# Projecting v and the output gate of a head together, 512 columns at a time

## The chip, the cores and the metric

The kernel runs on one core of a Trainium2 chip, as one launch. The metric is the device time in microseconds. The core's engines run side by side and meet at semaphores: TensorE (PE; matrix products into PSUM, and the loading of their stationary operand, PEld), VectorE (DVE), ScalarE (ACT), GpSimd (POOL) and SyncE (SP), which here only starts transfers.

## The reference

A trunk of two residual layers over 2048 tokens of width 1024: a chunked gated linear attention (GLA, 4 heads), then a causal convolution module, then one RMSNorm. The change touches the attention layer alone. Of that layer:

```python
proj = h @ w_in                       # h = rmsnorm(x, norm_w), (2048, 1024)
q, k, v, z, g_lr = jnp.split(
    proj, [GLA_DK, 2 * GLA_DK, 2 * GLA_DK + GLA_DV, 2 * GLA_DK + 2 * GLA_DV], axis=-1)
log_a = jax.nn.log_sigmoid((g_lr @ w_g2 + b_g).astype(jnp.float32)) / GLA_GATE_TAU
...
b = jnp.cumsum(log_a, axis=3)         # within a chunk of 64 tokens
q_dec = q * jnp.exp(b)
k_inv = k * jnp.exp(-b)
k_end = k * jnp.exp(b_last - b)
scores = jnp.where(causal, jnp.einsum('bhnid,bhnjd->bhnij', q_dec, k_inv), 0.0)
o_intra = jnp.einsum('bhnij,bhnjv->bhniv', scores, v)
# over the chunks: o_inter = q_dec @ S;  S = exp(b_last) * S + k_end^T v
...
o = o * lax.rsqrt(jnp.mean(o * o, axis=-1, keepdims=True) + EPS) * gn_w
o = o.reshape(B, T, GLA_DV) * jax.nn.silu(z)
x = x + o @ w_out
```

A head has 128 columns of q, 128 of k, 256 of v and 256 of z, the output gate.

## The kernel before

**Products.** Each float32 operand is split into a high and a low part (wh and wl for weights, ah and al for activations), and a product is the sum of three: high x high, high x low, low x high (`mm3`, line 144). `proj_f` takes 128 columns of the weights as the stationary operand and streams 512 tokens past them; q, k and the output projection go this way. `proj_t` takes 128 tokens as the stationary operand and streams 256 columns of the weights past them; v and z go this way. Either is 24 products (8 slices of the inner dimension, three each) into one PSUM bank.

**Weights.** The weight matrices are cut into units of 256 columns over all 1024 rows (8 KB per partition for each half of the split). A head has three: unit 3h for q and k, 3h+1 for v, 3h+2 for z; units 12 to 15 are the output projection, later ones belong to the convolution layer. `load_unit` brings one in two pieces of 512 KB: a transfer into `wr` (line 123, two buffers), a rounding copy on ScalarE to wh (124), a subtraction on GpSimd to wl (125; on VectorE for the first two units). wh and wl have two buffers each, and `next_unit` asks for one unit ahead.

**Order.** The sequence goes in two halves of 1024 tokens, each in two blocks of 512 (b = 0, 1) and eight groups of 128. `start_block` prepares a block: x is scaled and split (`prep_x`, 269 to 276), then `gate_low` makes the 16 columns of the gate's low rank (288; its weights `wgs` are split once at the start and stay in SBUF), the token norms (166 to 168, 178), and `gate` the factors E and Ei of a head (310 to 323). Then `head` runs over the four heads. `qk` makes q and k of a block and multiplies them by E and Ei out of PSUM (332, 338). `values` makes v of four groups (437, 438); all eight groups' v is kept (8 buffers). After that a loop over the eight groups makes z of a group (472) and issues the group's `core` in three stages, one unit of work apart: `scores` (379 to 383), `mix` (388 to 403) and `turn` (413 to 422). In head 0 of each half, block 0 has q, k and v made before block 1 is started. `out1` is the output projection with the residual, and starts block 0 of the next half (`ahead`).

**Banks.** PSUM's eight banks are in three groups: three of `mm` (projections), two of `pb`, three of `pm`. In head 0 v goes to `pb`, in the other heads to `mm`; `mix` uses `pb` throughout.

**What sets the order.** Tile's scheduler lists the instructions of each engine ahead of time, from their order in the program, their priorities (`tc.high_priority(offset=200)` moves those of `start_block` 200 places forward) and a simulated time line; a buffer is given out there as it comes free. On the chip each engine works through its list in order.

## Time and profile before

| | us |
|---|---|
| device time, median of 3 runs | 1694.59 (1694.3 to 1696.6) |
| span of the profiled execution | 1691.3 |
| TensorE busy in it | 1617.2 (96%) |
| VectorE | 1015.6 (60%) |
| GpSimd | 936.0 (55%) |
| ScalarE | 742.2 (44%) |

Times of instructions are from the span's start. The attention layer takes the first half of the span, to about 850 us, and the convolution layer the rest. Matmuls are pipelined: one's busy time overlaps the next one's, so that the cost of one in a full stream is the distance from start to start. A group of instructions is named by its line, engine, operation and output<-inputs; "idle before" is what the engine waited and for whom.

### The profile page before, as it was taken

What the parts mean: (1) busy time and instruction counts of PE and PEld (TensorE: products, weight loads), DVE (VectorE), ACT (ScalarE), POOL (GpSimd) and SP (SyncE); (2) the same over time, 40 slices, a digit from 0 to 9 for tenths busy, and PEclk for the clock granted to TensorE, in tenths of its full rate; (3) what the DMA queues carried; (4) which work ended last, traced back from release to release, by engine and by line L of the source; (5) the groups of instructions that cost most, each with busy time, mean ns of one, the idle gap of its engine ahead of it and who ended that gap; (6) DMA issues with size and microseconds to landing.
All of it is one profiled execution on the core that took longest, in us unless ns stands there. A gap on an engine that the chain in (4) does not pass through costs nothing.

```text
span 1691.3 us, 23564 instructions
## 1 busy us (share of the span) xinstructions
PE 1617.2 (96%) x9028; PEld 1413.4 (84%) x9028; DVE 1015.6 (60%) x1473; ACT 742.2 (44%) x1254; POOL 936.0 (55%) x795
## 2 busy tenths in 40 slices
...
GB/s 188 30 78 57 63 51 57 76 130 139 164 34 55 58 72 42 75 33 132 132 196 46 63 50 57 85 80 154 38 69 238 61 68 94 206 125 88 235 176 124
DMA packets 74015, 165.68 MB, mean 98 GB/s; under 512 B 7760, under 2 KB 16464, under 8 KB 73904
## 3 DMA queue, kind: packets, MB, share of 16 engines
...
q14 instruction: 41, 0.34, 0.1%
...
## 4 chain that ended last, share of the span: by engine, by line
PE 62%; DVE 16%; POOL 7%; DMA 6%; issue 4%; ACT 3%; SPq 0%; POOLq 0%; DVEq 0%; ACTq 0%
PE mm L144 52%; DVE pb L638 6%; PE pb L144 3%; DVE al L190 2%; DMA wr<-in_wall_dram 2%; PE pb L388 1%; POOL wl L125 1%; PE pb L390 1%; POOL convB L624 1%; DVE S L713 1%; PE pm L379 1%; POOL convA L624 1%; DVE d L734 1%; POOL b L736 1%; DVE pb L642 1%
## 5 line engine op out<-in xcount | busy, mean ns | idle before, releaser
L144 PE MATMUL mm<-ah,wh 128*128 128x512 f32 (+1 forms) x1600 | 599.1, 389 | 43.2 <-DVE u L761 10.7
L144 PE MATMUL mm<-al,wh 128*128 128x512 f32 (+1 forms) x1600 | 594.6, 387 | 1.7 <-DVE al L190 1.7
L144 PE MATMUL mm<-ah,wl 128*128 128x512 f32 (+1 forms) x1600 | 592.9, 387 | 2.3 <-POOL wl L125 2.3
L125 POOL TENSOR_TENSOR wl<-wr,wh 128x1024 fp32r<-128x1024 f32 x140 | 358.5, 2575 | 195.2 <-ACT wh L124 190.3
L144 PEld LDWEIGHTS mm<-ah,wh 128*128 128x128 f32 x1600 | 304.0, 191 | 109.0 <-DVE u L761 13.1
L144 PEld LDWEIGHTS mm<-ah,wl 128*128 128x128 f32 x1600 | 303.3, 191 | 62.4 <-POOL wl L125 4.2
L144 PEld LDWEIGHTS mm<-al,wh 128*128 128x128 f32 x1600 | 303.9, 191 | 59.7 <-DVE al L190 2.6
L144 PE MATMUL mm<-wh,ah 128*128 128x256 f32 x896 | 259.2, 289 | 0.0
L144 PE MATMUL mm<-wh,al 128*128 128x256 f32 x896 | 254.6, 284 | 0.0
L144 PE MATMUL mm<-wl,ah 128*128 128x256 f32 x896 | 254.2, 284 | 0.0
L124 ACT ACTIVATE wh<-wr 128x1024 fp32r<-128x1024 f32 x144 | 145.3, 1050 | 109.0 <-PE mm L144 78.9
L638 DVE SCALAR_TENSOR_TENSOR pb<-u,C,pb 128x512 f32<-128x512 f32 x252 | 183.8, 747 | 0.5
L638 DVE SCALAR_TENSOR_TENSOR pb<-u,dwc,pb 128x512 f32<-128x512 f32 x240 | 179.4, 748 | 1.6
L144 PEld LDWEIGHTS mm<-wl,ah 128*128 128x128 f32 x896 | 171.4, 191 | 0.4
L144 PEld LDWEIGHTS mm<-wh,ah 128*128 128x128 f32 x896 | 171.3, 191 | 0.4
L144 PEld LDWEIGHTS mm<-wh,al 128*128 128x128 f32 x896 | 171.3, 191 | 0.0
L622 ACT ACTIVATE prod<-u,C 128x512 f32<-128x512 f32 x148 | 105.6, 721 | 137.6 <-POOL convA L624 78.5
L624 POOL TENSOR_TENSOR convA<-convA,prod 128x512 f32<-128x512 f32 x74 | 99.5, 1344 | 6.6 <-ACT prod L622 3.0
L624 POOL TENSOR_TENSOR convB<-convB,prod 128x512 f32<-128x512 f32 x74 | 99.6, 1346 | 3.9 <-ACT convB L620 0.7
L397 DVE SCALAR_TENSOR_TENSOR S<-S,dec,pb 128x256 f32<-128x256 f32 x56 | 26.8, 479 | 95.4 <-PE pb L144 95.3
L401 POOL TENSOR_TENSOR ss<-ss,e 128x1 f32<-128x1 f32 x64 | 13.3, 208 | 124.5 <-ACT g L400 124.5
L523 DVE TENSOR_TENSOR Q<-mm,Q 128x512 f32<-128x512 f32 x32 | 22.0, 688 | 92.7 <-PE mm L144 78.9
...
## 6 DMA issues: line engine op xcount, KB each, us to landing
wr<-in_wall_dram SPq DMA_DIRECT2D x144, 512.0 KB, 4.1
...
```

What stands on the lines that cost most here:

```text
L124: act.activation(wh[:, ks, :], raw, AF.Copy)
L125: (dve if i < 2 else pool).tensor_tensor(wl[:, ks, :], raw, wh[:, ks, :].bitcast(F32), ALU.subtract)
L144: pe.matmul(ps, s, m, start=(i == 0), stop=(i == 3 * n - 1))
L190: dve.tensor_tensor(lo, src, hi.bitcast(F32), ALU.subtract)
L379: pe.matmul(s_ps[:, 0:192], ki[:, js], Q[:, j].rearrange("p s c -> p (s c)"), start=True, stop=True)
L388: pe.matmul(o_ps, Q[:, j, 0:2].rearrange("p s c -> p (s c)"), S[h], start=True, stop=False)
L390: pe.matmul(o_ps, x, y, start=first and n == 0, stop=n == 2)
L397: dve.scalar_tensor_tensor(S[h], S[h], dec[:, j:j + 1], kv, ALU.mult, ALU.add)
L523: dve.tensor_tensor(xr, ps, xr, ALU.add)
L622: act.activation(p, src, AF.Copy, scale=w)
L624: pool.tensor_tensor(acc, acc, p, ALU.add)
L638: dve.scalar_tensor_tensor(dstm, src, w, ps, ALU.mult, ALU.add)
```

## The change

v and z of a head become one projection of 512 columns. The weights of both lie side by side, and the two units now part the inner dimension: unit 3h+1 has its first 512 rows, unit 3h+2 the last 512, each of 512 columns (the same bytes). A group of 128 tokens is 24 products of 512 columns into one whole `mm` bank; v leaves the left half of the bank, Silu of z the right one, and the group's `core` stages follow at once. So v needs three buffers where it had eight. A wide pass holds both units from its first group to its last; units 0, 3, 6, 9 and 12 (q and k of each head, and the first of the output projection) get a pool of their own, `wq`, with one buffer. For the room this takes, `raw` has four buffers in place of five, and the gate's split weights no longer stay: they use a `wr` buffer, are written to DRAM once and read back for the three later blocks. In head 0, block 1 is started after the four groups of block 0; the gate of the next head is issued between groups 3 and 4.

```diff
...
 TAPS = 31
+UW = 2048
 HALO = 15
...
     order += list(range(28, 32)) * 4
+    LONE = {0, 3, 6, 9, 12}
     wstate = {"next": 0, "ready": []}
...
         u = order[i]
-        wh = wp.tile([P, KT, 256], F32R, name="wh")
-        wl = wp.tile([P, KT, 256], F32R, name="wl")
+        wpool = wq if u in LONE else wp
+        wh = wpool.tile([P, UW], F32R, name="wh")
+        wl = wpool.tile([P, UW], F32R, name="wl")
         wstate["ready"].append((u, wh, wl))
...
         def part(s):
-            ks = slice(4 * s, 4 * s + 4)
-            raw = wp.tile([P, 4, 256], F32, name="wr")
-            sp.dma_start(out=raw, in_=wall[u].rearrange("p (k c) -> p k c", c=256)[:, ks, :])
-            act.activation(wh[:, ks, :], raw, AF.Copy)
-            (dve if i < 2 else pool).tensor_tensor(wl[:, ks, :], raw, wh[:, ks, :].bitcast(F32), ALU.subtract)
+            cs = slice(s * UW // 2, (s + 1) * UW // 2)
+            raw = wp.tile([P, UW // 2], F32, name="wr", bufs=2)
+            sp.dma_start(out=raw, in_=wall[u][:, cs])
+            act.activation(wh[:, cs], raw, AF.Copy)
+            (dve if i < 2 else pool).tensor_tensor(wl[:, cs], raw, wh[:, cs].bitcast(F32), ALU.subtract)
...
-    def next_unit(expect):
-        while len(wstate["ready"]) < 2 and wstate["next"] < len(order):
+    def pop_unit(expect, ahead):
+        while len(wstate["ready"]) < ahead and wstate["next"] < len(order):
             load_unit()
...
         return wh, wl
+    def next_unit(expect):
+        return [w.rearrange("p (k c) -> p k c", c=256) for w in pop_unit(expect, 2)]
+    def next_wide(expect):
+        w = []
+        for s in range(2):
+            hl = [t.rearrange("p (k c) -> p k c", c=2 * DV) for t in pop_unit(expect + s, 3 - s)]
+            w += [(hl[0][:, k], hl[1][:, k]) for k in range(KT // 2)]
+        return w
...
     def proj_t(ps, w, a, j):
-        wh, wl = w
         s = slice(j * P, (j + 1) * P)
-        mm3(ps, [(a[k][0][:, s], a[k][1][:, s], wh[:, k, :], wl[:, k, :]) for k in range(KT)])
+        mm3(ps, [(a[k][0][:, s], a[k][1][:, s], w[k][0], w[k][1]) for k in range(KT)])
...
     l1 = ExitStack()
+    wq = l1.enter_context(tc.tile_pool(name="wq", bufs=1))
     s2 = l1.enter_context(tc.tile_pool(name="s2", bufs=1))
...
-    BUFS = {"raw": 5, "tmp": 3, "E": 2, "Ei": 2, "ki": 2, "kd": 1, "st": 4}
+    BUFS = {"raw": 4, "tmp": 3, "E": 2, "Ei": 2, "ki": 2, "kd": 1, "st": 4}
...
     S = [l1c.tile([P, DV], F32, name=f"S{h}") for h in range(HEADS)]
-    wgs = l1c.tile([P, KT, P], F32R, name="wgs")
     g2t = l1c.tile([96, HEADS * DK], F32R, name="g2t")
-    wgr = l1c.tile([P, KT, 16], F32, name="wgr")
+    wgd = tc.dram_tile((P, KT * P), F32, name="wg_scratch")
...
-    def load_small():
+    def gate_weights(first):
+        t = wp.tile([P, UW // 2], F32R, name="wr", bufs=2)
+        wgs = t.rearrange("p (k c) -> p k c", c=P)
+        if not first:
+            sp.dma_start(out=t.bitcast(F32), in_=wgd)
+            return wgs
+        wgr = t2("tmp")[:, 0:KT * 16].rearrange("p (k c) -> p k c", c=16)
         sp.dma_start(out=wgr, in_=wg)
...
             dve.tensor_tensor(wgv[:, :, r, 1, :], wgr, wgv[:, :, r, 0, :].bitcast(F32), ALU.subtract)
+        sp.dma_start(out=wgd, in_=t.bitcast(F32))
+        return wgs
...
-    def gate_low(hf, b, a, acc):
+    def gate_low(hf, b, a, acc, wgs):
         bank = m_bank if b == 0 else b_bank
...
-    def values(hf, h, w, a_b, b):
-        vs = []
-        for i in range(4 * b, 4 * b + 4):
-            ps = (b_bank() if h == 0 else mm_bank())[:, 0:DV]
-            proj_t(ps, w, a_b, i % 4)
-            vh, vl = (l1p.tile([P, DV], F32R, name=n, bufs=8) for n in ("vh", "vl"))
-            rr = r2[:, hf * 8 + i:hf * 8 + i + 1]
-            act.activation(vh, ps, AF.Copy, scale=rr)
-            dve.scalar_tensor_tensor(vl, ps, rr, vh.bitcast(F32), ALU.mult, ALU.subtract)
-            vs.append((vh, vl))
-        return vs
+    def values(hf, i, w, a_b):
+        ps = mm_bank()
+        proj_t(ps, w, a_b, i % 4)
+        q = hf * 8 + i
+        vh, vl = (l1p.tile([P, DV], F32R, name=n, bufs=3) for n in ("vh", "vl"))
+        act.activation(vh, ps[:, 0:DV], AF.Copy, scale=r2[:, q:q + 1])
+        dve.scalar_tensor_tensor(vl, ps[:, 0:DV], r2[:, q:q + 1], vh.bitcast(F32), ALU.mult, ALU.subtract)
+        sz = l1p.tile([P, DV], F32, name="sz", bufs=3)
+        act.activation(sz, ps[:, DV:2 * DV], AF.Silu, scale=rt[:, q:q + 1])
+        return (vh, vl), sz
...
         base = 3 * h
-        qkb, vs, nxt = [], [], None
-        if h == 0:
-            w = next_unit(base)
-            wv = next_unit(base + 1)
-            for b in range(2):
-                if b == 1:
-                    start_block(hf, b, a, EEs, g3s)
-                qkb.append(qk(h, w, a[b], EEs[b]))
-                if b == 1:
-                    nxt = gate(h + 1, g3s)
-                vs += values(hf, h, wv, a[b], b)
-        else:
-            w = next_unit(base)
-            for b in range(2):
-                run_late(1 if b == 0 else 0)
-                qkb.append(qk(h, w, a[b], EEs[b]))
-            w = next_unit(base + 1)
-            for b in range(2):
-                vs += values(hf, h, w, a[b], b)
-                if h < HEADS - 1 and b == 0:
-                    nxt = gate(h + 1, g3s)
-        w = next_unit(base + 2)
+        qkb, nxt, todo = [], None, []
         sink = {"stage": stage}
-        todo = []
-        for i in range(8):
-            ps = mm_bank()[:, 0:DV]
-            proj_t(ps, w, a[i // 4], i % 4)
-            sz = l1p.tile([P, DV], F32, name="sz", bufs=3)
-            act.activation(sz, ps, AF.Silu, scale=rt[:, hf * 8 + i:hf * 8 + i + 1])
-            todo.append(core(hf, h, i, vs[i], sz, qkb[i // 4], sink))
+        def tokens(i, w):
+            v, sz = values(hf, i, w, a[i // 4])
+            todo.append(core(hf, h, i, v, sz, qkb[i // 4], sink))
             todo[i][0]()
...
                 todo[i - 2][2]()
+        w = next_unit(base)
+        if h == 0:
+            qkb.append(qk(h, w, a[0], EEs[0]))
+            wv = next_wide(base + 1)
+            for i in range(4):
+                tokens(i, wv)
+            start_block(hf, 1, a, EEs, g3s)
+            qkb.append(qk(h, w, a[1], EEs[1]))
+        else:
+            for b in range(2):
+                run_late(1 if b == 0 else 0)
+                qkb.append(qk(h, w, a[b], EEs[b]))
+            wv = next_wide(base + 1)
+            for i in range(4):
+                tokens(i, wv)
+        if h < HEADS - 1:
+            nxt = gate(h + 1, g3s)
+        for i in range(4, 8):
+            tokens(i, wv)
         late.extend([todo[7][1], todo[6][2], todo[7][2]])
...
             a_b, acc = prep_x(hf, b, first_unit if hf == b == 0 else {})
+            wgs = first_wgs if hf == b == 0 else gate_weights(False)
             if hf == b == 0:
...
         with tc.high_priority(offset=offset):
-            g3 = gate_low(hf, b, a_b, acc)
+            g3 = gate_low(hf, b, a_b, acc, wgs)
             a.append(a_b)
...
     nxt = ([], [], [])
-    load_small()
+    first_wgs = gate_weights(True)
     part = load_unit()
...
         units.append(np.concatenate([w1[:, h * 128:(h + 1) * 128], w1[:, 512 + h * 128:512 + (h + 1) * 128]], 1))
-        units.append(w1[:, 1024 + h * 256:1024 + (h + 1) * 256])
-        units.append(w1[:, 2048 + h * 256:2048 + (h + 1) * 256])
+        vz = np.concatenate([w1[:, 1024 + h * 256:1024 + (h + 1) * 256], w1[:, 2048 + h * 256:2048 + (h + 1) * 256]], 1)
+        units += [vz[:512], vz[512:]]
     units += [wo1[:, j * 256:(j + 1) * 256] for j in range(4)]
...
     units += [wo2[:, j * 256:(j + 1) * 256] for j in range(4)]
-    wall = np.stack([u.reshape(KT, P, 256).transpose(1, 0, 2).reshape(P, KT * 256) for u in units])
+    wall = np.stack([u.reshape(-1, P, u.shape[1]).transpose(1, 0, 2).reshape(P, UW) for u in units])
...
```

## Rows read from the trace of the kernel before

**Rows 1.** Page, span and busy time of each engine (share of the span, instructions):

```profile
span 1691.3 us, 23564 instructions
...
PE 1617.2 (96%) x9028; PEld 1413.4 (84%) x9028; DVE 1015.6 (60%) x1473; ACT 742.2 (44%) x1254; POOL 936.0 (55%) x795
```

**Rows 2.** Stretches: us, busy time (instructions) of each engine, TensorE clock, DMA share, GB/s:

```profile
0.00:850.00 850.00, 836.71 (x5455) 768.79 (x5456) 301.06 (x549) 378.18 (x726) 350.10 (x404) 1.00 0.27 84
850.00:1691.00 841.00, 780.49 (x3575) 644.65 (x3573) 714.59 (x925) 363.98 (x528) 585.94 (x391) 0.97 0.34 112
```

**Rows 3.** Waits of PE up to 850 us: total us, times, longest; first and third of nine:

```profile
PE pm L288 <- ACT ah L270: 6.5, 1, 6.5
...
PE pb L144 <- DVE vl L438: 1.3, 1, 1.3
```

**Rows 4.** Groups by shape, up to 900 us: xcount, busy us, mean ns, idle before:

```profile
L144 PE MATMUL mm<-wh,ah 128*128 128x256 f32 x896 | 259.2, 289 | 0.0
...
L144 PE MATMUL mm<-ah,wh 128*128 128x512 f32 x536 | 210.3, 394 | 2.5 <-ACT wh L124 1.1 <-DVE Q L332 1.0 <-ACT ah L189 0.5
...
L144 PE MATMUL pb<-wh,ah 128*128 128x256 f32 x128 | 37.4, 294 | 1.3 <-DVE vl L438 1.3
```

**Rows 5.** Timeline of PE, a z group: start us, us, instruction; first and last of 27:

```profile
149.83 0.28 PE L144 MATMUL mm<-wh,ah 128*128 128x256 f32 x1
...
152.95 0.28 PE L144 MATMUL mm<-wh,al 128*128 128x256 f32 x1
```

**Rows 6.** Timeline of PE, output projection; first and last of 13:

```profile
399.67 0.39 PE L144 MATMUL mm<-ah,wh 128*128 128x512 f32 x1
...
402.39 0.39 PE L144 MATMUL mm<-ah,wh 128*128 128x512 f32 x1
```

**Rows 7.** DMA issues: xcount, KB each, median us from issue to landing:

```profile
wr<-in_wall_dram SPq DMA_DIRECT2D x144, 512.0 KB, 4.1
```

**Rows 8.** Groups by shape, up to 900 us: splitting of weights, emptying of v:

```profile
L125 POOL TENSOR_TENSOR wl<-wr,wh 128x1024 fp32r<-128x1024 f32 x64 | 157.1, 2470 | 96.3 <-ACT wh L124 96.3
...
L124 ACT ACTIVATE wh<-wr 128x1024 fp32r<-128x1024 f32 x68 | 68.3, 1052 | 46.1 <-PE mm L144 44.8 <-DMA wr<-in_wall_dram 1.2
...
L438 DVE SCALAR_TENSOR_TENSOR vl<-mm,r,vh 128x256 fp32r<-128x256 f32 x48 | 22.9, 483 | 89.3 <-ACT vh L437 89.2
...
L437 ACT ACTIVATE vh<-mm,r 128x256 fp32r<-128x256 f32 x48 | 22.1, 469 | 55.2 <-PE mm L144 55.2
```

**Rows 9.** Timeline of PE: last low-rank product, first of v, in block 0:

```profile
25.27 0.39 PE L288 MATMUL pm<-al,wgs 128*128 128x512 f32 x1
...
27.54 0.40 PE L144 MATMUL pb<-wh,ah 128*128 128x256 f32 x2
```

**Rows 10.** Timeline of DVE: the read of k's bank, block 0, first half:

```profile
48.35 0.69 DVE L338 TENSOR_TENSOR ki<-mm,Ei 128x512 f32<-128x512 f32 x1
```

**Rows 11.** Timeline of SP's queue at the start: issues of weight pieces:

```profile
13.84 0.33 SPq L123 DMA_DIRECT2D wr<-in_wall_dram  x1
...
23.53 2.73 SPq L123 DMA_DIRECT2D wr<-in_wall_dram  x2
```

**Rows 12.** Stretches of head 0, columns as in Rows 2:

```profile
27.50:48.00 20.50, 19.98 (x146) 18.84 (x144) 12.90 (x16) 12.63 (x20) 12.19 (x11) 1.00 0.15 50
459.50:484.00 24.50, 21.86 (x135) 20.42 (x135) 11.36 (x17) 14.57 (x22) 12.73 (x12) 0.86 0.13 42
474.20:481.00 6.80, 6.80 (x34) 6.80 (x33) 1.93 (x5) 6.02 (x7) 3.20 (x3) 0.50 0.00 1
```

**Rows 13.** Timeline of PE, second half, block 1: last projection, low-rank products' first and last:

```profile
490.89 0.39 PE L144 MATMUL mm<-ah,wl 128*128 128x512 f32 x1
...
492.03 0.47 PE L288 MATMUL pm<-ah,wgs 128*128 128x512 f32 x1
...
495.54 0.39 PE L288 MATMUL pm<-al,wgs 128*128 128x512 f32 x1
```

**Rows 14.** Timeline of DVE, second half, block 1: the read of k's bank:

```profile
508.10 0.69 DVE L338 TENSOR_TENSOR ki<-mm,Ei 128x512 f32<-128x512 f32 x1
```

## The prediction, made before the change had run

> **What bounds the kernel now.** I began with the busy shares and the span: TensorE's matmul row is busy 1617.2 of 1691.3 us, and the next engine, VectorE, 1015.6 [rows 1]. An average hides stages, so next I cut the span where the attention layer ends (the change touches only that layer). In the first 850 us TensorE is busy 836.71 us, VectorE 301, ScalarE 378, GpSimd 350, and the granted clock is 1.00 in the mean; in the rest VectorE and GpSimd come much closer [rows 2]. So in the stage that changes nothing but TensorE sets the time. The list of what TensorE waited for there has nine rows, the longest 6.5 us (the first activations) and the third already 1.3 [rows 3]. A microsecond taken out of TensorE's stream in this stage is a microsecond off the end, as long as no new gap opens.
>
> **What the stream is made of.** Busy time of matmuls overlaps, so I read starts, not durations. v and z are three forms of 896 products of 256 columns (two thirds of v, and all of z), and three of 128 that go to the other banks (v of head 0): 3 x (896 + 128) = 3072 [rows 4]. In a stretch where they run back to back, 27 starts cover 149.83 to 152.95, which is 3.12 / 26 = 120.0 ns each [rows 5]. The 512-column products of the same stage start every (402.39 - 399.67) / 12 = 226.7 ns [rows 6]. Two of 256 cost 240.0 ns, one of 512 costs 226.7: a fixed 13.3 ns goes with every product, whatever its width.
>
> **Term 1, the wider products: -20.4 us.** 3072 products become 1536, at 13.3 ns a pair: 1536 x 13.3 ns = 20.4 us, or 2.55 us in each of the 8 passes (four heads, two halves of the sequence). Nothing in these rows speaks for another pitch when activations are the loaded side: the 256-column form loads them already, and it has the same fixed part. Here the Trainium skill would say otherwise: TensorE: Matmul & The Clock Gate, section Back-to-back issue gap, gives an isolated gap of N / 2.4 + 2.5 ns, so 109.2 and 215.8 ns, and only 2.5 ns a pair, 3.8 us in all. The rows disagree with it at both widths (120.0 and 226.7), and I go by the rows.
>
> What surrounds the products stays in number: each group of tokens has still one scaled copy and one subtraction for v, one Silu for z, and the same three stages of its core. These stages now follow one group of 24 x 226.7 ns = 5.4 us apart, where a z group of 24 x 120.0 = 2.9 us lay between; their chain gets more room, and they cost TensorE what they did: zero.
>
> **Term 2, weights of heads 1 to 3: 0.** A wide pass holds both slots of the weight pool to its last product, so the next head's two wide units can only be split after that. The cover is that head's q and k: 4 x 24 x 226.7 ns = 21.8 us. The work is four pieces, each 1.05 us on ScalarE and 2.47 on GpSimd, and a transfer of 4.1 us [rows 7, 8]. Two raw pieces wait in their buffers beforehand; the other two follow as these come free. Two subtractions, a transfer, a copy and a subtraction, 2 x 2.47 + 4.1 + 1.05 + 2.47 = 12.6 us, some 15 with GpSimd's other work. Seven us of cover are left. If GpSimd were late by more, TensorE would wait by the excess; the first half of the rows is needed first, which gives 2.7 us more. Of the unit for q and k, which has a pool of its own, the loading lies beside the wide pass before.
>
> **Term 3, head 0 of the first half, block 0: +6 us (0 to +14).** Two facts meet here. First, q and k of a block stay in their PSUM banks until the gate's factors exist. Block 0's projections end at 27.5 us, and the last of the two banks is read at 48.4 to 49.0 [rows 9, 10]: for 21 us two of the three "mm" banks are taken. Before, v of head 0 went to the two "pb" banks in this time; now the wide group needs a whole "mm" bank, and one is left. A lone bank must be emptied between groups: copy 0.47 and subtraction 0.48 us, about 1.2 with the handing over [rows 8]. Second, the ring of two raw buffers now holds the gate's weights from the start until the last low-rank product at 25.3 [rows 9]. Before, the third piece was issued at 13.84, and the first two of the z unit at 23.53 and behind it [rows 11]. With one slot left, the second piece of unit 0 goes at 13.84, and each takes about 7 us (4.1 + 1.05 + a subtraction): the four pieces that the first wide group needs are ready at about 28, 33, 36 and 40. So it ends at about 41, the second at 41 + 1.2 + 5.4 = 47.6. TensorE was busy 19.98 of the 20.5 us from 27.5 to 48 [rows 12]. Now it has two wide groups, 10.9 us, and some 3 us of small products of gate and norm, 14 in all: 6 us idle that were not. The work is not lost, only later, but TensorE has no slack to take it up. At the low end the scheduler fills the hole with q and k of block 1; at the high end, which I estimate, pieces come 5 us later still, and the clock falls behind the hole as it does from 474.2 to 481, where 6.8 us at 0.50 cost 3.4 [rows 12]. I take +6, as worked.
>
> **Term 4, head 0, block 1, in both halves: +3.5 us each (0 to +20 each).** The gate's weights are now read back from DRAM for this block, into the same ring of two. In the order of the program unit 3 (q and k of head 1) asks for both slots just ahead, and it can't be split before q and k of block 1 have released unit 0. So the reload starts only after the last of those products, plus a copy and a subtraction (1.05 + 2.47), and takes 4.1 [rows 7, 8]. Then 16 low-rank products, 3.6 us, and the chain from the last of them to the end of the second read, 508.10 + 0.69 - 495.54 = 13.3 us, as it ran in the second half of the kernel before [rows 13, 14]. In sum 24.5 us after block 1's q and k, in which they hold two banks. Before, this chain began at once: the low-rank products follow the last projection within 1.4 us [rows 13]. What covers it: the four wide groups of block 1, 21.8 us, and the low-rank products, 3.6 us, are 25.4 us of work through one bank. They just suffice, but the lone bank costs about 1.2 us after each of three groups: 3.5. The 0 end: the reload gets a slot ahead of unit 3; below nothing it can't go, as the chain began at once before. The high end: 24.5 less 3.6 are some 20 us idle, if no wide group can run in that time. I take the near end, as one bank is free. The Trainium skill speaks against the change here: Perfetto Trace Analysis, section Matmuls, wants independent groups to rotate through PSUM banks so that emptying one overlaps the next group's products. The trace agrees as far as it goes: with two banks for v of head 0, TensorE waited for that subtraction once, 1.3 us [rows 3].
>
> **Term 5, head 0 of the second half, block 0: -2 us (-6 to +4).** From 459.5 to 484 the kernel before is itself not full: busy 21.86 of 24.5 at a mean clock of 0.86, the half clock standing from 474.2 to 481 [rows 12]. That is 2.6 us idle and 0.14 x 24.5 = 3.4 us of clock, 6 in all. The two banks of block 0 are held in the same way, so the wide groups run through one bank: three handings over of 1.2, about 4. It loses 4 in place of 6. At the ends nothing is lost, or 10 with the clock down for longer.
>
> **Small things: 0 (-3 to +3).** The first block's x tiles have four buffers for five, the split gate weights are written out once (0.5 MB) and read three times on SP's queue, a few more table loads fall on ScalarE (Silu between the gate's Exp and Ln), and the schedule of the convolution layer may shift. All of it lies on engines that are half idle [rows 2].
>
> **Sum.** -20.4 + 0 + 6 + 7 - 2 = -9.4 us. The profiled execution spans 1691.3 us, so 1681.9; the device time's median lies 3.3 us above that span, so 1685.2 us, 0.6% faster.
>
> **Rivals.** (a) Clean gain: the scheduler gives the gate's weights their slot early and fills the holes. For it: it has kept TensorE full through the same region in the first half (19.98 of 20.5 us). Against: q and k hold their banks in any order. It gives -20.4, less up to 6 for term 5: 1668 to 1678. (b) Gain eaten: the ends of terms 3 and 4 come half way, 10 and 2 x 6: about 0, 1691 to 1698. (c) Slower, by the ring of raw buffers: unit 3 sits in both slots, the gate of block 1 starts late, and no wide group runs in between, because they too lack a bank or their v buffers (three for eight). Its place is the end of q and k of block 1, in both halves; its price is 20 us each: -20.4 + 6 + 40 - 2 = +24, 1718. Since terms 1, 3 and 5 leave -16, it decides from 8 us in each half. (d) The products don't give 13.3 ns: the fixed part goes with every 256 columns that the weight tile streams and not with the product, so a wide one costs 240 ns. The q and k products speak against it, 512 columns at 226.7 ns [rows 6], but there the activations stream. Then term 1 is 0 and the sum +11: 1706. The Trainium skill's rule on the gap, above, comes near this: with its 2.5 ns the sum would be -3.8 + 11 = +7, 1702.
>
> **How the numbers follow.** Differences under 0.2% (3.4 us) can't be told from none. Forecast, gain partly given back (1678 to 1691.2): 0.50. (a) 0.22. (b) 0.14. (c) 0.12, half way to its full price included. (d) 0.02, as two rows speak against it. Faster 0.50 + 0.22 = 0.72, same 0.14, slower 0.14. The range, 1671 to 1701, leaves out the best of (a) and the full price of (c). The forecast's own range is 1678 to 1691.
>
> **What would show it.** Right on term 1: 512-column products with the activations loaded, 1536 of them at 226.7 ns from start to start, and none of 256 for v and z. Term 2: no wait of TensorE for a split weight at the head of a wide pass in heads 1 to 3. Term 3: a hole between 27 and 49 us ended by a weight piece or by v's subtraction. Term 4: the reload of the gate's weights issued only after unit 3's copy, some 7 us behind the last q and k product, and TensorE's gaps ended by v's subtraction. Wrong would be: a pitch above 235 ns, gaps in heads 1 to 3, or a second stage whose time moves by more than 5 us.

## The result: slower, and the profile after

The changed kernel takes 1719.78 us (median of 4 runs, 1717.68 to 1721.03) beside 1694.44 for the kernel before (4 runs): a ratio of 1.0157, interval 1.0139 to 1.0175. The forecast was 1685.2, range 1671 to 1701. The profiled execution spans 1715.9 us, against 1691.3 [rows 1]: 24.6 us more. The page's first rows (span; busy us, share, instructions):

```profile
span 1715.9 us, 20529 instructions
...
PE 1616.2 (94%) x7492; PEld 1336.8 (78%) x7492; DVE 1030.6 (60%) x1473; ACT 763.1 (44%) x1269; POOL 939.9 (55%) x795
```

TensorE's share fell from 96% to 94% on 1536 products fewer, and ScalarE's work grew by 21 us. The waits of PE up to 900 us (us in total, times, longest), beside [rows 3], name the new stops:

```profile
PE pm L334 <- DVE g L326: 8.0, 2, 7.0
...
PE mm L160 <- ACT sz L463: 6.0, 3, 4.1
PE mm L160 <- DVE Q L356: 3.5, 2, 1.8
PE mm L160 <- POOL wl L130: 2.9, 2, 1.9
PE pb L412 <- DVE S L421: 2.2, 4, 0.6
```

**The wide products are there.** There are three forms of 512 products of 512 columns, the activations loaded, in place of [rows 4]; of the groups by shape the first:

```profile
L160 PE MATMUL mm<-wh,ah 128*128 128x512 f32 x512 | 206.9, 404 | 10.7 <-ACT sz L463 6.0 <-DVE Q L356 3.5 <-ACT wh L129 1.2
```

A pitch is the distance from the start of one product to the start of the next. Two starts of the timeline of PE in head 1, second half, 16 products apart:

```profile
629.16 0.40 PE L160 MATMUL mm<-wl,ah 128*128 128x512 f32 x1
...
632.82 0.39 PE L160 MATMUL mm<-wh,al 128*128 128x512 f32 x1
```

(632.82 - 629.16) / 16 = 228.8 ns; over all pairs of heads 1 to 3 in the first half the median is 227.0 ns. The forecast's 226.7 holds.

**By stages.** Each head of each half has 96 products for q and k, so the 97th start of such a product opens head 1, and so on. The first products of head 1, of the output projection, of the second half, of its head 1, and of the convolution layer, after:

```profile
116.13 0.39 PE L160 MATMUL mm<-ah,wh 128*128 128x512 f32 x1
...
366.36 0.48 PE L160 MATMUL mm<-ah,wh 128*128 128x512 f32 x1
...
460.23 0.40 PE L160 MATMUL mm<-ah,wh 128*128 128x512 f32 x1
...
556.90 0.40 PE L160 MATMUL mm<-ah,wh 128*128 128x512 f32 x1
...
900.35 0.62 PE L160 MATMUL mm<-ah,wh 128*128 128x512 f32 x2
```

In the kernel before these five stand at 103.25, 352.91, 447.74, 540.60 and 883.13; its rows for head 1 in the first and the second half:

```profile
103.25 0.39 PE L144 MATMUL mm<-ah,wh 128*128 128x512 f32 x1
...
540.60 0.40 PE L144 MATMUL mm<-ah,wh 128*128 128x512 f32 x1
```

Each stretch splits into what its products need at full clock (13.3 ns and 0.417 ns a column, from the pitches of [rows 5, 6]) and the rest, which TensorE lost to waits, small gaps and half clock ("lost time" below). The stretches run from the first q and k product of one to that of the next. All in us:

| stretch | before | after | more | of it products | of it lost time |
|---|---|---|---|---|---|
| head 0, first half | 90.9 | 104.5 | +13.6 | 81.5 to 77.8 | 9.3 to 26.7 |
| heads 1 to 3, first half | 249.7 | 250.2 | +0.5 | 238.3 to 232.9 | 11.3 to 17.3 |
| head 0, second half | 92.9 | 96.7 | +3.8 | 79.8 to 76.1 | 13.0 to 20.6 |
| heads 1 to 3, second half | 250.8 | 252.6 | +1.8 | 238.7 to 233.1 | 12.4 to 19.6 |
| two output projections, and the start | 199.0 | 196.3 | -2.6 | | |
| convolution layer, to its last product | 795.0 | 802.3 | +7.3 | | |

The products gave 18.4 us (3.7 + 5.4 + 3.7 + 5.6); lost time took 38.2 in the same stretches (17.4 + 6.0 + 7.6 + 7.2), and the convolution layer, whose program is the same, 7.3.

**The two holes of head 0.** Windows over the stretches of [rows 12]:

```profile
27.50:48.00 20.50, 10.54 (x34) 6.11 (x33) 13.88 (x11) 14.82 (x22) 15.05 (x10) 0.78 0.45 151
459.50:484.00 24.50, 19.60 (x92) 15.64 (x91) 11.92 (x12) 12.07 (x19) 19.39 (x13) 0.98 0.50 164
```

TensorE is busy 10.54 us where it was busy 19.98, and the mean granted clock of this stretch is 0.78, where it was 1.00 [rows 12]. Timelines of ScalarE and, in the last two rows, of TensorE at the end of the first hole:

```profile
42.94 0.67 ACT L336 ACTIVATE tmp<-pm,C 128x512 f32<-128x512 f32 x1
43.64 0.63 ACT L340 ACTIVATE tmp<-tmp 128x512 f32<-128x512 f32 x1
44.29 1.28 ACT L342 ACT_TABLE_LOAD   x1
45.58 0.63 ACT L342 ACTIVATE tmp<-tmp 128x512 f32<-128x512 f32 x1
46.12 0.46 ACT L460 ACTIVATE vh<-mm,r 128x256 fp32r<-128x256 f32 x1
46.59 1.28 ACT L463 ACT_TABLE_LOAD   x1
47.89 0.47 ACT L463 ACTIVATE sz<-mm,rt 128x256 f32<-128x256 f32 x1
...
43.69 0.63 PE L160 MATMUL mm<-wh,al 128*128 128x512 f32 x1
...
48.42 0.80 PE L160 MATMUL mm<-wh,ah 128*128 128x512 f32 x1 [4.10 <-ACT sz L463]
```

The first wide group's last product starts at 43.69. Its lone bank is empty only after ScalarE has finished the gate's Exp (the Abs lay just before it), a table load and the Ln, and then the copy of v, another table load and the Silu of z. In the second half:

```profile
477.65 0.72 ACT L294 ACTIVATE ah<-raw,C 128x512 fp32r<-128x512 f32 x1 [3.91 <-DMA raw<-in_xT_dram]
...
478.85 0.39 PE L160 MATMUL mm<-wh,al 128*128 128x512 f32 x1
...
485.09 0.46 ACT L460 ACTIVATE vh<-mm,r 128x256 fp32r<-128x256 f32 x1
...
486.28 0.76 PE L334 MATMUL pm<-g,g2t 96*128 96x512 f32 x1 [7.04 <-DVE g L326]
```

The wide group ends at 478.85, and its v is copied 6.2 us later: ScalarE had stood for an x tile and had the splits to do first. The gate's input comes 26.0 us after the half's first q product (486.28 - 460.23). Before, it came as late, 26.1 us after it (473.84 - 447.74):

```profile
473.84 0.47 PE L310 MATMUL pm<-g,g2t 96*128 96x512 f32 x1 [1.37 <-DVE g L302]
```

but there v's products in the other two banks filled most of that time [rows 12].

### The profile page after: what moved, and what is told of

The parts are those of the page before. It is cut to its first block, busy times and chain, and to the rows that moved or that the text cites. A ratio compares the mean times of both kernels' runs of the same rounds, so it can differ in the third digit from the quotient of the medians.

```text
span 1715.9 us, 20529 instructions
## 1 busy us (share of the span) xinstructions
PE 1616.2 (94%) x7492; PEld 1336.8 (78%) x7492; DVE 1030.6 (60%) x1473; ACT 763.1 (44%) x1269; POOL 939.9 (55%) x795
## 4 chain that ended last, share of the span: by engine, by line
PE 54%; DVE 25%; ACT 6%; issue 5%; DMA 5%; POOL 5%; SPq 0%; POOLq 0%; DVEq 0%; ACTq 0%
PE mm L160 47%; DVE pb L659 12%; DVE pb L663 2%; DMA wr<-in_wall_dram 1%; DVE d L755 1%; PE pb L412 1%; PE pb L414 1%; PE pb L160 1%; PE pm L403 1%; DVE S L734 1%; DVE al L205 1%; DVE u L782 1%; POOL d L724 1%; POOL wl L130 1%; DVE al L295 1%
## 5 line engine op out<-in xcount | busy, mean ns | idle before, releaser
L130 POOL TENSOR_TENSOR wl<-wr,wh 128x1024 fp32r<-128x1024 f32 x140 | 352.3, 2527 | 161.7 <-ACT wh L129 152.0
L160 PE MATMUL mm<-wh,ah 128*128 128x512 f32 x512 | 206.9, 404 | 10.7 <-ACT sz L463 6.0
L160 PE MATMUL mm<-wl,ah 128*128 128x512 f32 x512 | 203.4, 397 | 4.1 <-POOL wl L130 2.9
L160 PE MATMUL mm<-wh,al 128*128 128x512 f32 x512 | 204.9, 400 | 0.0
L160 PEld LDWEIGHTS mm<-wh,ah 128*128 128x128 f32 x512 | 97.6, 191 | 32.4 <-ACT sz L463 7.1
L160 PEld LDWEIGHTS mm<-wl,ah 128*128 128x128 f32 x512 | 97.6, 191 | 24.6 <-POOL wl L130 3.9
L407 POOL TENSOR_TENSOR stl<-sT,sth 128x128 fp32r<-128x128 f32 x64 | 32.4, 507 | 146.7 <-ACT sth L406 146.7
L160 PEld LDWEIGHTS mm<-wh,al 128*128 128x128 f32 x512 | 97.5, 190 | 19.5
L645 POOL TENSOR_TENSOR convB<-convB,prod 128x512 f32<-128x512 f32 x74 | 99.5, 1345 | 8.5 <-ACT prod L643 4.5
L220 POOL TENSOR_TENSOR acc<-acc,kTl 128x512 f32<-128x512 f32 x28 | 37.7, 1348 | 81.6 <-ACT kTl L547 81.4
L461 DVE SCALAR_TENSOR_TENSOR vl<-mm,r,vh 128x256 fp32r<-128x256 f32 x64 | 30.9, 483 | 81.4 <-ACT vh L460 80.4
```

Source lines behind the costliest of these rows:

```text
L130: (dve if i < 2 else pool).tensor_tensor(wl[:, cs], raw, wh[:, cs].bitcast(F32), ALU.subtract)
L160: pe.matmul(ps, s, m, start=(i == 0), stop=(i == 3 * n - 1))
L220: eng.tensor_tensor(acc, acc, sq, ALU.add)
L407: pool.tensor_tensor(stl, st, sth.bitcast(F32), ALU.subtract)
L461: dve.scalar_tensor_tensor(vl, ps[:, 0:DV], r2[:, q:q + 1], vh.bitcast(F32), ALU.mult, ALU.subtract)
L645: pool.tensor_tensor(acc, acc, p, ALU.add)
```

## The experiments

"Over" is a run's median less that of the kernel before on the same chip. H0 and H1-3 are the stretches of head 0 and of heads 1 to 3, first and second half, "conv" is the convolution layer; all us. H0, H1-3 and conv are read from one profiled execution of each kernel, and single executions of one program spread by some us (the ten of e19 from 1687.36 to 1695.95), so that a difference of a few us between two of these columns is weak evidence.

| run | ratio and interval | over | H0 | H1-3 | conv |
|---|---|---|---|---|---|
| before | | | 90.9, 92.9 | 249.7, 250.8 | 795.0 |
| e19, before again | 1.0003 (0.9987 to 1.0018) | +0.1 | 91.7, 91.1 | 249.7, 250.8 | 793.7 |
| after | 1.0157 (1.0139 to 1.0175) | +25.3 | 104.5, 96.7 | 250.2, 252.6 | 802.3 |
| e3, narrow halves | 1.0331 (1.0301 to 1.0361) | +53.8 | 119.2, 108.9 | 252.2, 253.6 | 797.3 |
| e1, order of loads | 1.0186 (1.0165 to 1.0208) | +29.8 | 105.3, 103.9 | 247.8, 252.9 | 796.8 |
| e6, ring free at first | 1.0169 (1.0154 to 1.0185) | +27.3 | 106.7, 97.3 | 250.2, 252.6 | 798.2 |
| e2, other banks | 1.0173 (1.0146 to 1.0200) | +28.7 | 98.8, 89.6 | 257.8, 259.8 | 800.4 |
| e8, a fourth bank | 1.0120 (1.0092 to 1.0149) | +20.4 | 101.8, 92.3 | 257.3, 258.7 | 786.8 |
| e9, VectorE empties | 1.0165 (1.0141 to 1.0188) | +29.0 | 103.8, 99.9 | 249.3, 251.8 | 801.7 |
| e4, after with barrier | 1.0196 (1.0176 to 1.0216) | +32.4 | 103.6, 97.6 | 250.2, 252.6 | 792.4 |
| e5, before with barrier | 1.0093 (1.0066 to 1.0119) | +15.5 | 90.9, 92.7 | 249.6, 250.8 | 799.6 |
| e11, q and k first | 1.0199 (1.0173 to 1.0224) | +34.4 | 112.5, 108.7 | 247.2, 247.8 | 794.6 |
| e12, block 1 prepared early | 1.0378 (1.0349 to 1.0407) | +64.8 | 127.7, 123.5 | 244.6, 244.8 | 796.9 |
| e10, head 0 narrow, 4 buffers | 1.0253 (1.0225 to 1.0282) | +44.5 | 110.6, 109.7 | 248.9, 251.4 | 798.2 |
| e14, control with room | 1.0160 (1.0141 to 1.0179) | +25.3 | 102.1, 98.0 | 250.4, 252.7 | 795.9 |
| e13, head 0 as before | 1.0088 (1.0072 to 1.0104) | +14.1 | 99.5, 96.9 | 248.2, 249.2 | 795.5 |
| e15, wide groups run ahead | 1.0253 (1.0229 to 1.0277) | +43.5 | 91.0, 89.3 | 267.5, 266.0 | 806.7 |
| e16, e13 and gate resident | 1.0091 (1.0065 to 1.0117) | +15.9 | 98.5, 94.9 | 248.2, 249.2 | 798.0 |
| e17, e14 and gate resident | 1.0258 (1.0235 to 1.0281) | +43.4 | 108.2, 104.5 | 250.4, 252.8 | 799.2 |
| e18, e16 with two units | 1.0070 (1.0046 to 1.0095) | +10.8 | 95.9, 94.8 | 248.3, 249.3 | 797.0 |

A core stage of head 0 that slips behind head 1's first product counts in H1-3, so the two columns are read together. e13 to e18 compute something else than the reference, as said at e14.

### Is the width worth what was forecast? (e3)

```diff
-        proj_t(ps, w, a_b, i % 4)
+        for c in range(2):
+            cs = slice(c * DV, (c + 1) * DV)
+            proj_t(ps[:, cs], [(wh[:, cs], wl[:, cs]) for wh, wl in w], a_b, i % 4)
```

> Change against the changed kernel: a group is two accumulations of 24 products of 256 columns into the two halves of the same bank, all else (order, units, rings, buffers) as changed. It measures the wide product by itself. Theory: 13.3 ns a pair, 1536 pairs, 20.4 us slower, 1738 to 1742. Rival (in head 0 the products hide in the holes, so that only six passes of eight count): 15 us, 1733 to 1737. If width gave only 2.5 ns a pair: 1722 to 1725.

1744.73 us, a little above the theory's 1738 to 1742; its span is 24.3 us longer than the changed kernel's. By stages this isn't the sum that the theory added up. For 2.55 us a pass, head 0 would take 5.1 us more in its two passes, and heads 1 to 3 15.3 in their six. Measured are 26.9 more in head 0 (14.7 and 12.2), 3.0 in heads 1 to 3 (2.0 and 1.0), and 5.0 less in the convolution layer. So the total lies near 20.4 by chance. In heads 1 to 3, where TensorE has hardly a named wait, joining the products is worth 3 us and not 15: most of what the wider products gave there was lost again in small gaps. Why the narrow halves cost head 0 so much more than their products isn't shown.

### One suspected cost of head 0 at a time (e1, e6, e2, e8, e9)

**e1**: in head 0 the wide pass doesn't ask for unit 3 ahead of block 1's gate weights.

```diff
-    def next_wide(expect):
+    def next_wide(expect, ahead=3):
...
-            hl = [t.rearrange("p (k c) -> p k c", c=2 * DV) for t in pop_unit(expect + s, 3 - s)]
+            hl = [t.rearrange("p (k c) -> p k c", c=2 * DV) for t in pop_unit(expect + s, ahead - s)]
...
-            wv = next_wide(base + 1)
+            wv = next_wide(base + 1, 2)
```

> Change against the changed kernel: in head 0 the unit for q and k of head 1 (unit 3) is no longer asked for ahead of block 1's gate weights. Theory A (the ring of two raw buffers delays block 1's gate, and that costs): the reload follows the last q and k product of block 1 at once or comes before it, the 6.7 us between that product and the first low-rank one shrink to under 2, and the loss of block 1 (2.2 and 2.6 us over the kernel before) goes: 1714 to 1716 us. Theory B (the single free bank costs, the reload is hidden): the reload moves but the time stays within 1717 to 1722.

The edit moved the reload as meant: in the first half the low-rank products of block 1 now begin at 69.45 us, ahead of its last q and k product at 86.44. 1720.64 us and no shorter head 0 (the second one is 7.2 us longer): the order of unit 3 and the reload is not the loss.

**e6**: the first split gate weights are made in two `st` tiles, so that the ring of raw buffers is free from the start.

```diff
...
-        t = wp.tile([P, UW // 2], F32R, name="wr", bufs=2)
...
+            t = s2.tile([P, NB], F32R, name="st", bufs=BUFS["st"])
```

> Change against the changed kernel: the first block's split gate weights lie in two st buffers that are free then, so both raw buffers serve weight pieces from the start. Theory A (late pieces make the hole of the first half's block 0): the pieces of the first two wide units arrive some 5 to 7 us earlier and the loss of 17.7 us falls to about 10: 1711 to 1714. Theory B (the single bank, held until the gate's factors exist, makes the hole): the first group ends earlier but waits for its emptying behind the gate's chain, and the time stays within 1716 to 1721.

1718.16 us. The first stretch is 106.7: TensorE then waits for the Silu (10.7 us in the first 130) in place of the pieces. The late pieces hide behind the lone bank: theory B.

**e2**: the second and third wide group of each block of head 0 go to `pb` banks.

```diff
-        ps = mm_bank()
+        ps = b_bank() if h == 0 and i % 4 in (1, 2) else mm_bank()
```

> Change against the changed kernel: in head 0, groups 1, 2, 5 and 6 take a whole pb bank, so that three banks rotate while q and k hold two of the mm banks. Theory B (single bank): the time lost between the end of block 0's q and k and the start of block 1's, 17.7 us in the first half and 13.4 in the second, falls by some 6 and 6, and block 1's by 2 each: 1702 to 1706 us. Theory A (late weights and the ring): the first half's block 0 hardly moves, since its pieces arrive as late as before; 1713 to 1719.

**e8**: four `mm` banks, two `pm`.

```diff
-    ps_mm = ctx.enter_context(tc.tile_pool(name="ps_mm", bufs=3, space=bass.MemoryType.PSUM))
+    ps_mm = ctx.enter_context(tc.tile_pool(name="ps_mm", bufs=4, space=bass.MemoryType.PSUM))
...
-    ps_m = ctx.enter_context(tc.tile_pool(name="ps_m", bufs=3, space=bass.MemoryType.PSUM))
+    ps_m = ctx.enter_context(tc.tile_pool(name="ps_m", bufs=2, space=bass.MemoryType.PSUM))
```

> The changed kernel with four banks of the projections' pool in place of three and two of the small products' pool in place of three: a wide group may then wait for ScalarE's emptying while the next groups go on. Theory (the lone bank left to v and z in head 0 costs block 0 some 5 us in each half): block 0's lost time, 17.7 us in the first half and 13.4 in the second, falls by 4 to 6 us in each, and the whole is 1708 to 1713 us. Rival (TensorE waits for the emptying queue as such, or the small products miss the third bank): 1716 to 1722 us.

The wait that ends the second half's hole, 7.04 us in the changed kernel, in e2's timeline of PE:

```profile
488.71 0.47 PE L334 MATMUL pm<-g,g2t 96*128 96x512 f32 x1 [3.29 <-DVE g L326]
```

and in e8's:

```profile
491.39 0.47 PE L334 MATMUL pm<-g,g2t 96*128 96x512 f32 x1 [2.94 <-DVE g L326]
```

A further bank does fill that hole by about 4 us: there the lone bank is part of the cause. But the attention layer isn't shorter: both pay 6 to 8 us per half in heads 1 to 3, so that head 0 to 3 take 356.6 and 349.4 us in e2, 359.1 and 351.0 in e8, against 354.7 and 349.3. e2's total of 1719.59 is above both its bands. e8's total of 1709.96 is in its expected band for another reason: its convolution layer is 15.5 us shorter.

**e9**: VectorE takes v and z out of the bank in head 0, the Silu follows from SBUF.

```diff
+        if h == 0:
+            dve.tensor_scalar(sz, ps[:, DV:2 * DV], rt[:, q:q + 1], None, ALU.mult)
+            dve.tensor_scalar(vh, ps[:, 0:DV], r2[:, q:q + 1], None, ALU.mult)
...
+        if h == 0:
+            act.activation(sz, sz, AF.Silu)
...
```

> The changed kernel, but in head 0 VectorE empties the bank of v and z (v scaled, z scaled into SBUF) and ScalarE takes the Silu from SBUF afterwards. Theory (ScalarE's queue, with the gate's chain and its table loads ahead of the emptying, holds the bank): TensorE's waits for the Silu of head 0 (4.1 us in the first half, and the stretch ended by the 7.0 us wait in the second) go, and the whole is 1708 to 1713 us. Rival (the gate's chain itself, ended by k's product against it, or the late weights set the end of block 0): the waits move to other rows and the whole is 1716 to 1721 us.

The two holes end so in e9 (timeline of PE):

```profile
45.66 0.76 PE L160 MATMUL mm<-wh,ah 128*128 128x512 f32 x1 [1.65 <-DVE vl L466]
...
485.14 0.76 PE L334 MATMUL pm<-g,g2t 96*128 96x512 f32 x1 [6.77 <-DVE g L326]
```

The emptying in the first half falls from 4.10 to 1.65 us, so most of that wait was ScalarE's queue. The second hole stays, and the whole is 1718.47: the rival's side.

### Is the convolution layer's share the change's? (e4, e5, e19)

e4 and e5 put one line between the layers, e19 is the kernel before unchanged.

```diff
     l1.close()
+    tc.strict_bb_all_engine_barrier()
```

> The changed kernel with one barrier of all engines between the attention layer and the convolution layer, so that no step of the second is scheduled among those of the first. Theory (the attention layer loses 17 us, the convolution layer's further 7 us come from the order in which the scheduler put unchanged work): beside the kernel before with the same barrier this one ends 16 to 19 us later, and the two convolution layers, taken from their first product to the last, are within 1.5 us of each other. Rival (the convolution layer itself suffers from the change, through the weights' buffers): its length differs by 6 to 8 us as it does without the barrier, and the whole by 23 to 26 us.

> The kernel before with the same barrier of all engines between the layers. Theory: a few us over the kernel before (1693 to 1706), and 16 to 19 us below the changed kernel with the barrier. Rival: 23 to 26 us below it.

> The kernel before, unchanged, as its own second profile: how far the length of a stretch moves between two executions of the same program. Theory (stages that nothing changed move by a few us): head 0's and heads 1 to 3's stretches within 1 us of the first profile, the convolution layer (795.0 us there) within 5 us, the whole within 0.3% of the kernel before. Rival (an execution repeats to within 1 us): the 7 us of the convolution layer then belong to the change.

With the barrier, the convolution layer's instructions on ScalarE and GpSimd stand in the same order in both kernels but for one step, VectorE's but for two, and TensorE's products differ in order in some more places. The difference is 1721.92 - 1705.06 = 16.9 us, in the band of the theory; but the theory's second mark fails, since the layer's lengths, 792.4 and 799.6, differ by 7 us the other way, where it wanted 1.5. Part of this can be the execution that was profiled: the four of e5 spread from 1701.28 to 1709.28, and its profile is of the slowest. e19's profile repeats every stretch within 2 us. The same part of different programs varies from 787 to 807 us, on both sides of 795. So nothing here ties the 7.3 us to the wide weights; that they come from the scheduler's order is possible, not shown.

### Other orders of head 0 (e11, e12, e10)

**e11**: q and k of both blocks ahead of v and z. **e12**: block 1 prepared behind the first wide group.

```diff
             qkb.append(qk(h, w, a[0], EEs[0]))
+            start_block(hf, 1, a, EEs, g3s)
+            qkb.append(qk(h, w, a[1], EEs[1]))
             wv = next_wide(base + 1)
```

> The changed kernel with v and z of 512 columns, but in head 0 q and k of both blocks come ahead of any v and z, as in heads 1 to 3. Theory (in the kernel before, products of block 1's q and k and of v in other banks filled block 0's waits; the change put block 1 behind block 0's four wide groups and took that filling away): head 0's first stretch falls from 104.4 to 92 to 98 us, its second is 93 to 97, and the whole lies 10 to 18 us over the kernel before. Rival (too few banks: q and k of block 1 have no bank until the gate of block 0 is ready, and the products of v and z start still later): head 0's stretches stay at 104 and 97 us or grow, the whole 25 us and more over.

```diff
             for i in range(4):
+                if i == 1:
+                    start_block(hf, 1, a, EEs, g3s)
                 tokens(i, wv)
-            start_block(hf, 1, a, EEs, g3s)
```

> The changed kernel with block 1 of head 0 prepared (loads, splits, norm, gate) right behind block 0's first wide group in place of behind its fourth; q and k of block 1 stay where they are. Theory (what is missing is filling for block 0, not an earlier gate of block 1): block 0's loss stays, block 1's falls by at most 2 us a half, the whole 20 to 27 us over the kernel before. Rival (the late start of block 1 is the loss): 8 to 16 us over.

The longest wait of PE in e11, in block 0 (timeline):

```profile
52.68 0.77 PE L160 MATMUL mm<-ah,wh 128*128 128x512 f32 x1 [7.46 <-DVE Q L356]
```

and in e12, in block 1:

```profile
88.06 0.80 PE L312 MATMUL pm<-ah,wr 128*128 128x512 f32 x1 [6.56 <-DMA wr<-wg_scratch]
```

e11 is the rival: q of block 1 has no bank until block 0's gate lets Q be read. e12 lies beyond both expectations: the low-rank products now stand in TensorE's list ahead of a reload that isn't there yet.

**e10**: head 0 narrow again, v through `pb`, but only four buffers for v (and two for sz), so that v of block 1 can't run ahead.

```diff
+            vs += [values_narrow(hf, i, wv, a[0]) for i in range(4)]
             start_block(hf, 1, a, EEs, g3s)
             qkb.append(qk(h, w, a[1], EEs[1]))
...
+            for i in range(4):
+                tokens(i, wz)
+            nxt = gate(h + 1, g3s)
+            vs += [values_narrow(hf, i, wv, a[1]) for i in range(4, 8)]
```

> The change undone in head 0 alone, as far as memory allows: head 0 takes v in groups of 256 columns through the other pool's two banks, then q and k of block 1, then z in groups of 256 (v of block 1 after block 0's z, since only four groups of v fit); heads 1 to 3 stay as changed. Theory (head 0 loses 13.5 us in the first half and 3.8 in the second, and heads 1 to 3 gain nothing net): head 0's two stretches fall from 104.4 and 96.7 us to 91 to 96 each, and the whole lies 0 to 10 us over the kernel before. Rival (the loss comes from the order of loads and of unchanged work, which head 0's shape does not touch): 20 us and more over the kernel before.

1734.28 us, 44.5 over: the theory missed, and the time lies in the rival's band. Narrow products and the old banks alone don't bring head 0 back; but block 1's v and the order also differ here from the kernel before.

### With room for the buffers (e14, e13, e15, e16, e17, e18)

To make room, e14 leaves out the low part of the weights: it is still computed, but TensorE reads the high part in its place, so that e14 and the five built on it (e13, e15 to e18) give another sum than the reference, with as many products of the same shapes. This frees 16 KB a partition.

```diff
-        wl = wpool.tile([P, UW], F32R, name="wl")
-        wstate["ready"].append((u, wh, wl))
+        wstate["ready"].append((u, wh, wh))
...
-            (dve if i < 2 else pool).tensor_tensor(wl[:, cs], raw, wh[:, cs].bitcast(F32), ALU.subtract)
+            wx = wp.tile([P, UW // 2], F32R, name="wx", bufs=2)
+            (dve if i < 2 else pool).tensor_tensor(wx, raw, wh[:, cs].bitcast(F32), ALU.subtract)
```

> A control that makes room: the low parts of the weights (all but the gate's) are still computed, but into a small scratch tile, and TensorE reads the high part in their place (so what is computed is not the reference's sum: the term of the activations with the low part of the weights is replaced by one more of the high part). Count and shape of the products stay. It frees 16 KB a partition and nothing else is changed from the changed kernel. Theory: 22 to 31 us over the kernel before, as the changed kernel, with the same stretches of head 0 (104 and 97 us). If the low parts' lateness were the loss it would lie under 18.

25.3 us over, as the changed kernel: a fair control.

**e13**: head 0 is the code of the kernel before, eight buffers for v.

```diff
+            for b in range(2):
+                if b == 1:
+                    start_block(hf, b, a, EEs, g3s)
+                qkb.append(qk(h, w, a[b], EEs[b]))
...
+                vs += values_narrow(hf, wv, a[b], b)
```

> In the room of that control (the low parts of the weights replaced by the high ones, as there), head 0 exactly as in the kernel before: v of both blocks in groups of 256 through the two other banks into eight buffers, q and k of block 1 between them, then z with the cores; heads 1 to 3 of 512 columns as changed. Theory (head 0's loss is that v no longer runs ahead of the gate): head 0's stretches are 90 to 94 and 92 to 95 us as before the change, heads 1 to 3 stay within 2 us of the kernel before, and the whole is 3 us under to 8 us over it. Rival (a new resource, the loads or the buffers of the weights, costs it): 15 us and more over.

11 us back of the control's 25, none of the two expectations in full: 8.6 and 4.0 us of head 0 are left. Of those 11, the profile has 3.7 in head 0's stretches and 5.7 in heads 1 to 3, where cores of head 0 may lie; but v has eight buffers in the wide heads too here, where the control has three, so the two causes aren't parted.

**e15**: wide groups, three of them ahead of block 1, six buffers.

```diff
+            for i in range(3):
+                vs[i] = values(hf, h, i, wv, a[0])
             start_block(hf, 1, a, EEs, g3s)
             qkb.append(qk(h, w, a[1], EEs[1]))
```

> In the same room, head 0 with groups of 512 columns that run ahead: three groups (two of them in the other pool's banks) are projected and emptied before block 1's q and k, into six buffers in place of three, and each core follows its group three groups later. Theory (it is the running ahead that the change took, not the width): head 0's stretches are 92 to 99 and 91 to 95 us, the whole 2 to 14 us over the kernel before. Rival (a wide group in head 0 is late whatever its buffers, by its weights and its emptying): stretches of 102 and 96 us or more, 18 us and more over.

Head 0's stretches fall to 91.0 and 89.3, as short as the theory asked or shorter, and the whole rises by 18 us over the control. Not all of this is head 1: from head 0 to 3 the two halves take 6.0 and 4.6 us more than the control's, and the convolution layer 10.8. Windows of e15 before and behind head 1's start (columns as in [rows 2]):

```profile
12.00:104.00 92.00, 81.96 (x356) 66.62 (x357) 38.29 (x51) 53.86 (x75) 33.14 (x27) 0.98 0.28 91
104.00:122.00 18.00, 10.51 (x47) 8.48 (x45) 7.08 (x12) 13.11 (x22) 16.57 (x15) 0.79 0.33 109
```

and its timeline of PE there:

```profile
113.39 0.38 PE L414 MATMUL pb<-vh,stl 128*128 128x256 f32 x1 [1.85 <-POOL stl L407]
...
114.93 1.22 PE L412 MATMUL pb<-S,Q 128*128 128x256 f32 x2 [1.04 <-DVE S L419]
...
121.39 0.58 PE L160 MATMUL pb<-vh,kTh 128*128 128x256 f32 x1 [4.60 <-DVE g L427]
```

From 111 us on the last cores follow one another with no projection between them: TensorE is busy 10.51 of 18 us. As I read it, a wide group can fill the gate's time or the cores' time, not both; before, v filled the one and z the other.

**e16** and **e17**: gate's weights in a tile of their own, five x buffers, on e13 and on e14.

```diff
+    wgs_keep = l1c.tile([P, KT, P], F32R, name="wgs_keep")
...
-            sp.dma_start(out=t.bitcast(F32), in_=wgd)
-            return wgs
+            return wgs_keep
```

> As e13 (head 0 as before the change; the low parts of the weights replaced by the high ones in TensorE's products, to make room), and now the gate's split weights stay in a tile of their own and the x tiles have five buffers again. Of the change only the wide products of heads 1 to 3, with their weights, are left. e13 left 8.6 us of head 0's first stretch and 4.0 of the second. Theory (these come from the gate's weights in the ring of raw buffers, with ScalarE waiting 8.0 us for the broadcast behind them): head 0's stretches are 90 to 94 and 92 to 95 us, the whole 6 us under to 5 us over the kernel before. Rival (they come from the loading of two units for head 1's wide pass beside head 0): 98 and 96 us as in e13, 10 us and more over.

> As the control e14 (head 0 wide as changed, the low parts of the weights replaced by the high ones in TensorE's products), and now the gate's split weights stay in a tile of their own and the x tiles have five buffers again: no gate weights pass through the ring. Theory (of head 0's loss, 13.5 and 3.8 us, the ring holds 8.6 and 4.0, as e13 left): head 0's stretches fall from the control's 102 and 98 us to 93 to 97 and 93 to 96, the whole lies 8 to 18 us over the kernel before. Rival (the ring costs the wide head 0 nothing, since its wait for banks is longer): 102 and 98 us again, 21 us and more over.

e16's first stretch, 98.5, and its whole, 15.9 over, are the rival's: the ring isn't what e13 left there. The second stretch, 94.9, is 2.0 below e13's and inside the theory's band. e17 is worse than its control by 18 us, worse than even the rival had it; TensorE waits longer for the lone bank (timeline):

```profile
43.31 1.22 PE L160 MATMUL mm<-wh,ah 128*128 128x512 f32 x2 [7.70 <-ACT sz L458]
...
56.39 1.22 PE L160 MATMUL mm<-wh,ah 128*128 128x512 f32 x2 [5.44 <-ACT sz L458]
```

**e18**: as e16, and head 0's first unit rotates with the others.

```diff
-    LONE = {0, 3, 6, 9, 12}
+    LONE = {3, 6, 9, 12}
```

> As e16 (head 0 as before, gate's weights in a tile of their own, wide heads 1 to 3, the low parts of the weights replaced by the high ones in TensorE's products), and the unit of q and k of head 0 shares the two rotating buffers with v and z as before the change, so that the z unit can't be split on GpSimd while block 0's gate is under way. e16 left 7.6 us of head 0's first stretch and 2.0 of the second; GpSimd was busy 14.0 us of the 15 from 30 to 45 us there, against 8.9 before. Theory (the third buffer lets the weights' subtractions run ahead of the gate's own step on GpSimd): head 0's stretches are 90 to 94 and 92 to 94 us, and the whole falls by 4 to 9 us below e16, to 7 to 12 us over the kernel before. Rival (they come from the wide units of head 1): 98 and 95 us as in e16.

The stretch from 30 to 45 us in e16 (columns as in [rows 2]):

```profile
30.00:45.00 15.00, 15.00 (x104) 13.85 (x103) 6.76 (x8) 8.28 (x16) 14.02 (x10) 1.00 0.28 98
```

and in e18:

```profile
30.00:45.00 15.00, 15.00 (x114) 14.40 (x114) 8.89 (x12) 8.98 (x15) 8.75 (x7) 1.00 0.11 36
```

GpSimd's busy time falls from 14.02 to 8.75 us and the first stretch by 2.6, to 95.9, between the two expectations; the second stays at 94.8. The whole lies 10.8 over in place of 15.9, but the intervals of e16 (1.0065 to 1.0117) and e18 (1.0046 to 1.0095) overlap, so that only the 2.6 us are read here. The third weight buffer, which lets the subtractions in ahead of the gate's step, is a small part, as far as these runs tell. No kernel here beats the kernel before.

## Why the prediction was wrong

**Right.** Term 1, as a price of the products alone: 18.4 of the 20.4 us, at 228.8 ns in the stretch shown. The Trainium skill's gap of an isolated product (TensorE: Matmul & The Clock Gate, Back-to-back issue gap) gives 215.8 ns as an estimate; the trace disagrees. Term 2 as far as it speaks of weights: TensorE waited for no weight in heads 1 to 3. Term 4 in its size: the losses behind 84 us are 4.6 us, in the second half behind 524 us 5.5, small as forecast (3.5 each on top of the old losses). But they weren't ended by v's subtraction, as the term had it: the named waits in either are mainly one of 1.8 us for the read of q's bank (DVE Q) and one of 0.9 for the Silu. The reload is issued 3.8 us behind the last q and k product (3.5 told), and the low-rank products begin 6.9 us behind it (7.6 told); timeline of PE and SP's queue:

```profile
83.93 0.40 PE L160 MATMUL mm<-ah,wl 128*128 128x512 f32 x1
...
87.71 0.32 SPq L258 DMA_DIRECT2D wr<-wg_scratch  x1
...
90.85 0.50 PE L312 MATMUL pm<-ah,wr 128*128 128x512 f32 x1 [0.15 <-DMA wr<-wg_scratch]
```

**Term 3, sized too low.** Head 0 of the first half lost 17.4 us more than before, where terms 3 and 4 had 9.5. The step that failed: "about 1.2 with the handing over". It counted the copy and the subtraction of v and left out the Silu of z, which empties the same bank and is what TensorE waited for; the table loads stood among the small things. A bank is handed over when ScalarE's list comes to it, and the list had the end of the gate's chain and two table loads of 1.28 us in it: 4.10 us. e9 took 2.5 us of it away by using another engine. The pieces were late as told (waits of up to 1.94 us) but hid behind this (e6). From 27.5 to 48 TensorE stood idle 10.0 us, 9.4 more than before, where the term had 6, and the clock was down (0.78 in the mean), which it had only at its high end.

**Term 5, wrong in sign.** Forecast -2, and with term 4 +1.5; measured +7.6. It priced three handings over. What came is one hole of 7.04 us: the gate's input is 26 us away, and with q, k and one wide group TensorE has three banks full after 18.6. e2 and e8 fill 4 us of it with a bank more.

**"They cost TensorE what they did: zero", wrong.** In heads 1 to 3 products fell by 11 us in all and lost time rose by 13.2. The sum had nothing for this. e3 says how much hangs on the width: with narrow halves in the same structure the products of heads 1 to 3 grow back, and the time there grows by 3.0 us only. Waits that the profile names are a small part; one, in head 1 of the second half:

```profile
632.15 1.23 DVE L344 TENSOR_TENSOR_SCAN Ei<-scanm,Ei 128x512 f32<-128x512 f32 x1 [3.79 <-POOL Ei L343]
...
633.29 0.46 DVE L421 SCALAR_TENSOR_TENSOR S<-S,dec,pb 128x256 f32<-128x256 f32 x1
...
633.80 0.70 PE L412 MATMUL pb<-S,Q 128*128 128x256 f32 x2 [0.59 <-DVE S L421]
```

The update of S stands behind the next head's scan in VectorE's list, and TensorE waits for S. The rest are gaps below 0.4 us (15.1 and 16.4 us, 11.3 and 12.4 before), over half of it beside a small product of gate or core, the rest between products of the projections. e13, e16 and e18 have the wide heads beside an old head 0 and gain only 1.4 to 1.6 us a half there. What makes these gaps stays open. Gaps in heads 1 to 3 were one of the prediction's own signs of being wrong, a second stage that moves by more than 5 us another.

**Small things: 0 ±3, too narrow.** The convolution layer took 7.3 us more; its cause is open.

**The sum.** -18.4 and +17.4, +7.6, +13.2 of lost time, +7.3 of the convolution layer, -2.6 of the output projections and the start: +24.5 of the 24.6 us.

**The rivals.** (c) said 1718, near the result, by another mechanism: unit 3 in both raw buffers, with 20 us at the end of block 1's q and k. The loss there is 5 us, e1 changes the order without gain, and e17 takes the gate's weights out of the ring and is slower. Its number was right by chance. (d) falls with the pitch: 227 to 229 ns, not 240. (a) gave a range up to 1678, which its own sum, -20.4 less up to 6, doesn't reach: 1668 to 1674. What the runs support in its place for head 0: in the kernel before, v of head 0 was work that needed neither the gate nor a free `mm` bank, and z was left to lie between the cores. Joining them takes the first away; that this is the mechanism is argued from e13 and e15, not measured by itself. In the first half, twelve kernels with a wide head 0 take 352.5 to 372.3 us from the first q product to the output projection, and e3 lies among them; the three with the old head 0 and its eight buffers 344.2 to 347.7; the kernel before 340.6. With four buffers (e10) it is 359.5. So the old head 0, with the eight buffers that came along, brings back 9 to 11 of the 25 us (e13 and e16 against e14), and the third weight buffer may account for 2.6 us more in the first stretch (e18 against e16). The 11 us that e18 still lies over the kernel before aren't resolved, and the open part is larger than that: the wide products of its heads 1 to 3 alone should have put it some 11 us below.

The Trainium skill's rule that independent groups should rotate through banks (Perfetto Trace Analysis, Matmuls) bears on this change: the second half's hole agrees (7.04 us to 2.94 with a bank more), but as shown the attention layer as a whole doesn't get shorter.
